# Every feed-forward part opens with a plain pair of gate and up tiles; the ys copy and the next sums go ahead of splits

## Chip, core and metric

The kernel runs on one core of a Trainium2 chip. The metric is the time of one launch on the device in microseconds (us). Three timed runs of the kernel before gave 2052.0, 2054.82 and 2058.25 us, median 2054.82 us.

## What is computed

Two layers act on a hidden state of 512 tokens by 1024 channels, f32. In each layer four parts are added to it, and an RMS norm ends the whole:

```python
h += 1/2 * SwiGLU_1(rmsnorm(h))        # feed-forward, 1024 -> 2816 -> 1024
u  = rmsnorm(h) @ w_in                 # mixer: RG-LRU, windowed attention, gated DeltaNet
h += concat(A, B, C) @ w_out
h += 1/2 * SwiGLU_2(rmsnorm(h))        # second feed-forward
h += sigmoid(rmsnorm(h) @ w_ple_gate) * (p[l] @ w_ple_proj)

def rms_norm(x, g):
    y = x * rsqrt(mean(x * x, axis=-1) + EPS)
    return y * g

def swiglu(x, w_gate, w_up, w_down):
    return (silu(x @ w_gate) * (x @ w_up)) @ w_down
```

There are thus four feed-forward parts: F1 and F2 of layer 0, F1 and F2 of layer 1.

## The kernel before

The hidden state stays in SBUF, transposed, as `hT`: eight tiles of 128 channels by 512 tokens, called d = 0 to 7 here and taken in the order PAIRED = 0, 4, 1, 5, 2, 6, 3, 7. Products are as precise as f32: each operand is split into a high part (rounded to fp32r by ScalarE, ACT) and a low part (the rest, by VectorE, DVE), and each product takes three matmuls: high x high, high x low, low x high. The norm's factor per token is applied after the products; the gain is multiplied in at the split (`gained`, L247).

**A feed-forward part** (`ffn`, L357) makes 22 units: for each of 11 blocks of 256 hidden channels one gate unit (g) and one up unit (u). A unit (`Unit`, L537) is a 2x2 block product by Strassen-Winograd's scheme: seven block products p2, p1, p3, p7, p6, p4, p5 in place of eight, of 4 x 3 = 12 matmuls of 256 columns each, so 84. It needs sums of blocks on both sides. The sums of the weights (s2, s4, and one made by an accumulating DMA from GpSimd's queue into `r`) and their splits, in four groups a, b, c, d, are made by ACT and DVE while the unit before runs. The sums of hT's blocks ("t1", "t2", "T3", "T4", "B22") are made once for each part by `upper` (L272) and `lower` (L285), as hT's tiles get their last value: in the mixer for F2 and in `ple` for F1 of layer 1. So the tail of the stage before makes all operands, and the first pair (`first_pair`, L630) is a Strassen pair whose first products need the last tile of hT after 18 matmuls of 256 columns.

F1 of layer 0 opens otherwise, with `plain_pair` (L692): four plain tiles (g0, g1, u0, u1) of 24 matmuls of 512 columns, that need only the splits of hT, into X tiles; the sums, and the squares for the norm, which DVE adds up in `acc` (L308), follow behind.

PSUM tile Y of a unit holds p3 and p7; p4 adds to its half. ACT must have copied Y to `ys` (p37, L556) before p4 starts on TensorE (PE), and `e` (p16, L560) before p5, which runs inside the next unit. Each engine executes its own list in order. Within a part's rounds PE, ACT and DVE have the order in which the code stands (`manual_schedule`), with splits of down weights between them where a scheduler put them. Round 0 covers blocks 0 to 4 and round 1 blocks 5 to 10; after a round come the down products (pd), whose weights are split in `chunk` and `end`. A round's last unit has no unit to prepare; it loads and splits the first two chunks (`made[0]`, `made[1]`).

The gating of a pair (`Gating`, L480) is spread over the next units: scale (DVE), silu (ACT), mult (DVE), hi (ACT), lo (DVE). Weights of the next part are started early by the generator `ahead`: each `next(ahead)` in the mixer (L879) and in `ple` (L1578) runs one piece of the next part's opening. At the very end `out` multiplies by the norm's row, in part on GpSimd (POOL).

Of the kernel before, what the change touches and what calls it, by code (L numbers as in the profile page):

```python
# [9 lines left out]
F32 = mybir.dt.float32  # L10
# [31 lines left out]


AT0 = (-1, 2)
AT1 = (7, 11)
# [17 lines left out]
def trunk(ctx: ExitStack, tc: tile.TileContext, a):  # L63
# [168 lines left out]
    class Norm:  # L232


        def __init__(self, gain, combined):
            self.gain = gain
            self.acc = per.tile([128, S], F32, tag="acc", name="acc")
            self.x = None
            if combined:
                self.x = Combined()  # L240
                self.raw = {}
                self.neg = per.tile([128, KD], F32, tag="neg", name="neg")
                V.tensor_scalar(out=self.neg, in0=gain, scalar1=-1.0, scalar2=None, op0=ALU.mult)
# [10 lines left out]
        def split(self, k, t512, cs=ALL):  # L254
            if not self.x:
                self.gained(k, cs, self.xh[k][:, cs], self.xl[k][:, cs])
            elif k < 4:
                if cs.stop == S:
                    self.plain(k, cs)
                    self.upper(k, t512)  # L260
            else:
                self.plain(k, cs)
                self.lower(k - 4, cs)

        def plain(self, k, cs=ALL):
            x = self.x
            if k < 4 and hasattr(x, "first"):
                for i in range(2):
                    A.activation(out=x(i, "B11", k), in_=x.first[k][:, i, H:S].bitcast(F32), func=AF.Copy)
            elif k < 4:  # L270
                self.gained(k, HALVES[1], x(0, "B11", k), x(1, "B11", k))
            else:  # L272
                self.gained(k, cs, x.both(0, 0, k - 4)[:, cs], x.both(1, 0, k - 4)[:, cs])

        def upper(self, q, t512):
            x, h, gk = self.x, hT[:, q, :], self.gain[:, q:q + 1]
            g, t14, t32 = t512("tg"), t512("t14"), t512("t32")
            self.raw[q] = g, t14, t32
            A.activation(out=g[:, 0:H], in_=h[:, 0:H], func=AF.Copy, scale=gk)
            V.scalar_tensor_tensor(out=t14[:, 0:H], in0=h[:, H:S], scalar=gk, in1=g[:, 0:H],  # L280
                                   op0=ALU.mult, op1=ALU.subtract)
            split(t14[:, 0:H], x(0, "t1", q), x(1, "t1", q))

        def lower(self, q, cs=ALL):
            x, h = self.x, hT[:, q + 4, :]  # L285
            gk, nk = self.gain[:, q + 4:q + 5], self.neg[:, q + 4:q + 5]
            g, t14, t32 = self.raw[q]
            if cs.start == 0:

                V.scalar_tensor_tensor(out=t32[:, 0:H], in0=h[:, 0:H], scalar=gk, in1=g[:, 0:H],  # L290
                                       op0=ALU.mult, op1=ALU.subtract)
                V.scalar_tensor_tensor(out=t32[:, H:S], in0=h[:, 0:H], scalar=nk, in1=t14[:, 0:H],
                                       op0=ALU.mult, op1=ALU.subtract)
                split(t32, x.both(0, 1, q), x.both(1, 1, q))
            if cs.stop == S:

                V.scalar_tensor_tensor(out=t14[:, H:S], in0=h[:, H:S], scalar=nk, in1=t32[:, H:S],
                                       op0=ALU.mult, op1=ALU.subtract)
                split(t14[:, H:S], x(0, "T4", q), x(1, "T4", q))

        def square(self, k, t512, cs=ALL):
            h, acc = hT[:, k, cs], self.acc[:, cs]
            if k == 0:
# [6 lines left out]
        def add(self, k, t512):  # L310
            if k == 0:
                self.take_operand()
            self.split(k, t512)
            self.square(k, t512)

        def sums(self, t512, cs=ALL):
            n = (cs.stop - cs.start) // 128
            ps = bank([128, NT, 2], "ssc")
            for t in range(n):
# [9 lines left out]
            for x in (rh, rl):  # L329
# [4 lines left out]
                dg = t512("sq", F32R)[:, cs]  # L334
# [22 lines left out]
    def ffn(l, which, at=AT1):  # L357
        with ExitStack() as es:
# [37 lines left out]
            def load(u):  # L396
                j, m = units[u]
                src = a[f"{m}{which}"][l, j]
                if u not in raw1:
                    raw1[u] = loaded(src[:, 0:8], 8)  # L400
                    if u:
                        raw3[u] = wrp.tile([128, 8, 128], F32, tag="wr", name="wr")
                    else:

# [1414 lines left out]
```

## Time and profile before

| | |
|---|---|
| profiled execution, whole | 2052.92 us |
| its span, first to last instruction | 2051.1 us |
| timed runs, median of 3 | 2054.82 us |
| PE busy | 1967.7 us, 96% |
| DVE busy | 1509.4 us, 74% |
| ACT busy | 1002.0 us, 49% |

PE is the bound nearly everywhere. To read on: where PE has idle time, what it waits for, and what in ACT's or DVE's list stands ahead of that. Records of PE overlap: a matmul's record is longer than the step from its start to the next start, so steps are taken from starts.

### The profile page before, as it was taken

Reading aid. Unit: us, or ns where it says so; the run is one execution under the profiler, and the core shown is the slowest. Engines: PE = TensorE matmul, PEld = TensorE weight load, DVE = VectorE, ACT = ScalarE, POOL = GpSimd, SP = SyncE. Lnnn points to the kernel's source line nnn. Section 1 sums busy time; section 2 is a strip of 40 time slices with the busy share of each in tenths; the row PEclk is TensorE's granted clock in tenths of the full one; section 3 lists DMA queues with packets and bytes.
Section 4 is the critical chain, followed back from the end, with each engine's and each line's share of the span. In section 5 each row is a group of like instructions: output and inputs, shape, how many; then the busy total and the mean of one; then the engine's idle time right before and its main releaser. Section 6 shows DMA issues by size and latency. Waiting matters only on the chain.

```text
span 2051.1 us, 32033 instructions
## 1 busy us (share of the span) xinstructions
PE 1967.7 (96%) x12625; PEld 1752.2 (85%) x12625; DVE 1509.4 (74%) x2620; ACT 1002.0 (49%) x1651; POOL 181.2 (9%) x197
## 2 busy tenths in 40 slices
PE   7999999999999999999989999999899999999996
PEld 5988998887778989997879899988677899899885
DVE  7875883879878856865888568647897887488466
ACT  5642652454745534643556336434366565156343
POOL 0100000042201000000000000000421000000001
PEclk8999999999999999999999999999999999999998
DMA  6763743221046745643457357322111377275411
GB/s 193 194 172 95 188 129 113 78 73 47 17 124 171 188 120 147 174 126 103 124 136 189 114 148 186 124 83 96 53 42 44 117 201 192 76 188 139 136 62 62
DMA packets 85415, 254.51 MB, mean 124 GB/s; under 512 B 9616, under 2 KB 17040, under 8 KB 85008
## 3 DMA queue, kind: packets, MB, share of 16 engines
q1 hardware_dynamic: 72880, 207.36, 31.8%
q0 software_dynamic: 12384, 45.09, 12.5%
q8 instruction: 99, 1.62, 0.3%
q14 instruction: 52, 0.43, 0.1%
HBM read 250.32 MB, written 2.10 MB: 123 GB/s over the span
## 4 chain that ended last, share of the span: by engine, by line
PE 75%; DVE 16%; ACT 4%; issue 3%; DMA 1%; SPq 0%; DVEq 0%; ACTq 0%
PE pu L475 10%; PE pg L475 10%; PE pd L147 8%; PE pd L149 8%; PE qu L475 8%; PE pd L148 8%; PE qg L475 7%; PE pp L147 2%; PE pp L148 1%; PE pp L149 1%; PE ppg L149 1%; PE ppg L148 1%; PE ppg L147 1%; DVE wl L124 1%; DVE gl L443 1%
## 5 line engine op out<-in xcount | busy, mean ns | idle before, releaser
L475 PE MATMUL pu<-T,gh 128*128 128x256 f32 x880 | 159.5, 280 | 0.0
L475 PE MATMUL pg<-T,gh 128*128 128x256 f32 x784 | 144.4, 282 | 9.5 <-ACT T L251 7.5
L443 DVE TENSOR_TENSOR gl<-wr,gh 128x1024 fp32r<-128x1024 f32 x102 | 124.6, 1221 | 26.6 <-ACT gh L438 26.6
L123 ACT ACTIVATE wh<-wr 128x1024 fp32r<-128x1024 f32 (+2 forms) x76 | 77.2, 1015 | 135.1 <-PE pp L148 50.5
L475 PEld LDWEIGHTS pu<-T,gh 128*128 128x128 f32 x880 | 134.7, 188 | 0.0
L129 DVE TENSOR_TENSOR gl<-wr,gh 128x1024 fp32r<-128x1024 f32 x53 | 64.5, 1223 | 93.6 <-ACT gh L128 93.4
L475 PEld LDWEIGHTS pg<-T,gh 128*128 128x128 f32 x784 | 121.2, 189 | 11.1 <-ACT T L251 8.1
L147 PE MATMUL pd<-X,gh 128*128 128x512 f32 x328 | 128.8, 393 | 0.0
L149 PE MATMUL pd<-X,gl 128*128 128x512 f32 x328 | 128.7, 392 | 0.0
L148 PE MATMUL pd<-X,gh 128*128 128x512 f32 x328 | 127.8, 390 | 0.0
L475 PE MATMUL pu<-T,gl 128*128 128x256 f32 x440 | 123.0, 279 | 0.0
L438 ACT ACTIVATE gh<-wr 128x1024 fp32r<-128x1024 f32 x102 | 105.2, 1046 | 19.9 <-PE pd L148 14.0
L128 ACT ACTIVATE gh<-wr 128x1024 fp32r<-128x1024 f32 x53 | 55.8, 1059 | 120.7 <-PE pd L148 95.2
L475 PE MATMUL pg<-T,gl 128*128 128x256 f32 x392 | 110.1, 281 | 0.0
L475 PE MATMUL pg<-T,wh 128*128 128x256 f32 x592 | 107.3, 280 | 2.3 <-DVE cg L554 2.3
L124 DVE TENSOR_TENSOR wl<-wr,wh 128x1024 fp32r<-128x1024 f32 (+2 forms) x64 | 74.1, 1157 | 40.9 <-ACT wh L123 40.2
L147 PE MATMUL pp<-X,wh 128*128 128x512 f32 x240 | 102.1, 425 | 0.0
L438 ACT ACTIVATE sh<-r 128x512 fp32r<-128x512 f32 x80 | 50.6, 632 | 103.6 <-DVE r L455 103.6
L149 PE MATMUL pp<-X,wl 128*128 128x512 f32 x240 | 98.2, 409 | 2.0 <-DVE wl L124 2.0
L443 DVE TENSOR_TENSOR wl<-wr,wh 128x1024 fp32r<-128x1024 f32 x67 | 81.8, 1221 | 23.4 <-ACT wh L438 23.4
L148 PE MATMUL pp<-X,wh 128*128 128x512 f32 x240 | 98.2, 409 | 0.2 <-DVE X L252 0.2
L475 PEld LDWEIGHTS pg<-T,wh 128*128 128x128 f32 x592 | 90.5, 188 | 3.2 <-DVE cg L554 2.9
(477 smaller groups left out, 6048.9 us busy)
## 6 DMA issues: line engine op xcount, KB each, us to landing
wr<-in_d_dram SPq DMA_DIRECT2D x64, 512.0 KB, 3.9
wr<-in_g_dram SPq DMA_DIRECT2D x45, 512.0 KB, 4.3
wr<-in_u_dram SPq DMA_DIRECT2D x45, 512.0 KB, 4.3
r<-in_g_dram SPq DMA_DIRECT2D x43, 512.0 KB, 3.7
r<-in_u_dram SPq DMA_DIRECT2D x43, 512.0 KB, 4.1
r<-in_g_dram POOLq DMA_DIRECT2D x43, 512.0 KB, 7.3
r<-in_u_dram POOLq DMA_DIRECT2D x43, 512.0 KB, 6.9
wr<-in_wi_dram SPq DMA_DIRECT2D x30, 512.0 KB, 3.3
```

The lines of the kernel that those rows point to most:

```text
L123: A.activation(out=hi, in_=raw, func=AF.Copy)
L124: (via or V).tensor_tensor(out=lo, in0=raw, in1=hi.bitcast(F32), op=ALU.subtract)
L128: A.activation(out=hi, in_=x, func=AF.Copy)
L129: V.tensor_tensor(out=lo, in0=x, in1=hi.bitcast(F32), op=ALU.subtract)
L147: T.matmul(out=out, lhsT=wh, rhs=xh, start=start, stop=False)
L148: T.matmul(out=out, lhsT=wh, rhs=xl, start=False, stop=False)
L149: T.matmul(out=out, lhsT=wl, rhs=xh, start=False, stop=stop)
L438: A.activation(out=self.g[n][0], in_=self.of(n)[0], func=AF.Copy)
L443: V.tensor_tensor(out=g[1], in0=raw, in1=g[0].bitcast(F32), op=ALU.subtract)
L475: T.matmul(out=ps, lhsT=l_[:, q, :], rhs=r_, start=start and q == 0 and i == 0, stop=stop and q == 3 and i == 2, skip_group_check=more)
```

## The change

1. All four parts open with `plain_pair`. Its operands are the splits of hT in T tiles; the right half of the columns of d = 0 to 3 stands in "B11", the left in "T4", so these blocks take two matmuls of 256 columns in place of one of 512. The tails of the mixer and of `ple` split the plain weights of the next part's first pair (four groups) and hT; the sums of hT's blocks (`sums_of`) are made inside the pair by DVE and ACT, and the last sum, which takes T4's place, behind its last tile. `first_pair` is gone.
2. In F1 of layer 0 the squares are no longer added by DVE: `summed` adds them on PE, 4 matmuls of 2 columns for each d. In the other parts DVE still adds them.
3. In each unit `p37`, the copy to `ys`, goes ahead of the split of group c; `lo` of the pair goes behind that of group a. In a round's last unit `made[1]` goes behind `e`, and the first `end` is made there.
4. `out` multiplies by pairs of tiles on DVE alone; POOL no longer takes part. A tile named dg of its own holds the norm's diagonal, in place of one shared with sq.

```diff
-            if not self.x: ...
-            elif k < 4:
-                if cs.stop == S:
-                    self.plain(k, cs)
-                    self.upper(k, t512)
+            elif k < 4:
+                for half, name in zip(HALVES, ("T4", "B11")):
+                    if cs.start <= half.start and half.stop <= cs.stop:
+                        self.gained(k, half, self.x(0, name, k), self.x(1, name, k))
...
+        def sums_of(self, q, t14, t512):
+            h, h4, g = hT[:, q, :], hT[:, q + 4, :], t512("tg", q)
...
+            A.activation(out=g[:, 0:H], in_=h[:, 0:H], func=AF.Copy, scale=gk)
+            for out, a_, k, b in ((t14[:, 0:H], h[:, H:S], gk, g[:, 0:H]), (t32[:, 0:H], h4[:, 0:H], g4, g[:, 0:H]),
+                                  (t32[:, H:S], h4[:, 0:H], n4, t14[:, 0:H]), (t14[:, H:S], h4[:, H:S], n4, t32[:, H:S])):
+                V.scalar_tensor_tensor(out=out, in0=a_, scalar=k, in1=b, op0=ALU.mult, op1=ALU.subtract)
+            parts = (t14[:, 0:H], [self.x(i, "t1", q) for i in range(2)]), (t32, [self.x.both(i, 1, q) for i in range(2)])
+            for t, (hi, lo) in parts:
+                A.activation(out=hi, in_=t, func=AF.Copy)
...
+            def last():
+                split(t14[:, H:S], self.x(0, "T4", q), self.x(1, "T4", q))
...
+        def summed(self, k, sq):
+            for t in range(NT):
+                T.matmul(out=self.ps[:, t, :], lhsT=sq[:, 128 * t:128 * t + 128], rhs=ones[:, 0:2],
+                         start=k == PAIRED[0] and t == 0, stop=k == PAIRED[-1], skip_group_check=True)
...
+                tile("g", 0)
+                combine(0)
+                combine(1)
+                more[0][0]()
+                squares(PAIRED[0:2])
+                combine(2)
+                more[1][0]()
+                squares(PAIRED[2:4])
                 w.part("a")
+                tile("g", 1)
+                summed(PAIRED[0:4])
+                combine(3)
+                more[2][0]()
+                squares(PAIRED[4:6])
                 w.s2()
+                more[3][0]()
+                squares(PAIRED[6:8])
                 w.part("b")
+                tile("u", 0)
+                summed(PAIRED[4:8])
                 norm.sums(t512)
                 w.s4()
                 w.part("d")
                 w.part("c")
+                tile("u", 1)
+                for _, last in more:
+                    last()
                 return None, None, PlainGating(ps, into(0, 0))
...
                         unit.p(7)
+                        unit.p37()
                         if w:
                             w.room("c")
                             w.hi("c")
-                        unit.p37()
...
                         unit.p16()
+                        if not w:
+                            made[1] = grouped(raws[1], 8)
...
                         unit.c21()
+                        if not w and r == 0:
+                            make_end(0)
...
-                    for i in range(2):
-                        if k + i < n:
-                            V.tensor_tensor(out=o[:, i, :], in0=hT[:, k + i, cs], in1=pr, op=ALU.mult)
-                        else:
-                            G.tensor_tensor(out=o[:, i, :], in0=hT[:, k + i, cs], in1=rb, op=ALU.mult)
+                    V.tensor_tensor(out=o, in0=hT[:, k:k + 2, cs], in1=pr.unsqueeze(1).to_broadcast([128, 2, S // 2]),
+                                    op=ALU.mult)
```

DVE's list at the seam from the mixer of layer 0 to F2, before, from the last tile of hT (L1571) on. `t_` are sums, `T_` their splits, `acc` the squares.

```order
L1571 TENSOR_TENSOR hT<-hT,pwo 128x512
L129 TENSOR_TENSOR T_6035<-t_6030,T_6034 128x256
L290 SCALAR_TENSOR_TENSOR t_6031<-hT,par,tg 128x256
L292 SCALAR_TENSOR_TENSOR t_6031<-hT,neg,t_6030 128x256
L252 SCALAR_TENSOR_TENSOR T_6072<-hT,par,T_6071 128x512
L297 SCALAR_TENSOR_TENSOR t_6030<-hT,neg,t_6031 128x256
L308 TENSOR_TENSOR acc<-acc,sq 128x512
L129 TENSOR_TENSOR T_6078<-t_6031,T_6077 128x512
L243 TENSOR_SCALAR neg<-par 128x8
L129 TENSOR_TENSOR T_6035<-t_6030,T_6034 128x256
L554 TENSOR_TENSOR cg<-cg,pg 128x256
```

The same place after (the tile's last value is made in L1517; `X_6096` to `X_6099` hold sums, `wl` is a split of the plain pair's weights).

```order
L1517 TENSOR_TENSOR hT<-hT,pwo 128x512
L272 SCALAR_TENSOR_TENSOR X_6099<-hT,par,X_6098 128x256
L272 SCALAR_TENSOR_TENSOR X_6099<-hT,neg,X_6096 128x256
L247 SCALAR_TENSOR_TENSOR T_6076<-hT,par,T_6075 128x512
L272 SCALAR_TENSOR_TENSOR X_6096<-hT,neg,X_6099 128x256
L298 TENSOR_TENSOR acc<-acc,sq 128x512
L272 SCALAR_TENSOR_TENSOR X_6096<-hT,par,X_6098 128x256
L272 SCALAR_TENSOR_TENSOR X_6099<-hT,par,X_6098 128x256
L272 SCALAR_TENSOR_TENSOR X_6099<-hT,neg,X_6096 128x256
L272 SCALAR_TENSOR_TENSOR X_6096<-hT,neg,X_6099 128x256
L279 TENSOR_TENSOR T_5844<-X_6096,T_5843 128x256
L279 TENSOR_TENSOR T_6143<-X_6099,T_6142 128x512
```

Before, the sums that need the last tile (L290, L292, L297) stand around its own split (L252), and the splits of these sums (L129) follow at once. After, its split (L247) comes third, the sums (L272) follow it as part of a longer list, pair of tiles by pair, and the splits of T4 (L129) are not among the rows.

ACT's list in the gate unit of the second pair of F2, layer 0, before: splits (L438), the copy to ys (L558), and silu (L500) of the pair before.

```order
L438 ACTIVATE gh<-r_6365 128x1024
L500 ACT_TABLE_LOAD
L500 ACTIVATE th<-cg 128x512 x2
L553 ACTIVATE cg<-pg 128x256
L438 ACTIVATE sh<-r_6365 128x512
L438 ACTIVATE wh<-wr 128x1024
L438 ACTIVATE gh<-wr 128x1024
L558 ACTIVATE ys<-qg 128x512
L562 ACTIVATE e<-pg 128x256
```

The same after: the copy is L539, splits are L429, silu is L509.

```order
L429 ACTIVATE wh<-r_6344 128x1024
L534 ACTIVATE cg<-pg 128x256
L429 ACTIVATE sh<-r_6344 128x512
L429 ACTIVATE gh<-wr 128x1024
L341 ACTIVATE rb<-prow 128x512
L539 ACTIVATE ys<-qg 128x512
L429 ACTIVATE wh<-wr 128x1024
L509 ACT_TABLE_LOAD
L509 ACTIVATE th<-gs 128x512 x2
L543 ACTIVATE e<-pg 128x256
```

Here the silus and their table load stand behind ys, and one split in place of two stands between sh and ys, with the copy of the norm's row (`rb`).

ACT's list in the last unit of round 0 in F1 of layer 0, before: L128 splits down weights.

```order
L553 ACTIVATE cu<-pu 128x256
L128 ACTIVATE gh<-wr 128x1024
L128 ACTIVATE wh<-wr 128x1024
L128 ACTIVATE sh<-wr 128x512
L558 ACTIVATE ys<-qu 128x512
L562 ACTIVATE e<-pu 128x256
L128 ACTIVATE gh<-wr 128x1024
L128 ACTIVATE sh<-wr 128x512
L128 ACTIVATE gh<-wr 128x1024
```

The same after (L124 splits down weights, L539 copies to ys).

```order
L534 ACTIVATE cu<-pu 128x256
L124 ACTIVATE gh<-wr 128x1024
L539 ACTIVATE ys<-qu 128x512
L543 ACTIVATE e<-pu 128x256
L124 ACTIVATE wh<-wr 128x1024
L124 ACTIVATE sh<-wr 128x512
```

One split of down weights is left between cu and ys; the two that followed it now come behind e.

## Rows read from the trace of the kernel before

**Rows 1.** The page, part 1: engine, busy us (share of the span) x instructions.

```profile
PE 1967.7 (96%) x12625; PEld 1752.2 (85%) x12625; DVE 1509.4 (74%) x2620; ACT 1002.0 (49%) x1651; POOL 181.2 (9%) x197
```

**Rows 2.** Waits of PE: engine line <- releaser: us in total, times, longest us.

```profile
PE qg L475 <- ACT ys L558: 9.3, 8, 2.0
PE qg L475 <- ACT sh L438: 8.6, 1, 8.6
...
PE pg L475 <- ACT T L251: 7.5, 3, 6.3
...
PE qu L475 <- ACT ys L558: 6.6, 5, 1.6
```

**Rows 3.** Timeline, PE, F1 of layer 0: start, us, what [idle before <-releaser].

```profile
9.02 0.80 PE L147 MATMUL pg<-X,gh 128*128 128x512 f32 x1 [3.33 <-ACT gh L128]
...
23.65 0.39 PE L147 MATMUL pu<-X,gh 128*128 128x512 f32 x1
...
34.41 0.40 PE L149 MATMUL pu<-T,wl 128*128 128x512 f32 x1
...
70.18 0.40 PE L475 MATMUL pg<-T,gh 128*128 128x256 f32 x2
```

**Rows 4.** The chain that ended last, two units: start us, us, what.

```profile
70.34 2.83 PE pg L475 x24
...
80.23 2.83 PE pu L475 x24
```

**Rows 5.** Timeline, PE, F2 of layer 0.

```profile
620.04 0.39 PE L475 MATMUL pg<-T,gh 128*128 128x256 f32 x2
...
622.87 0.38 PE L475 MATMUL pg<-T,gh 128*128 128x256 f32 x1 [0.64 <-ACT T L251]
...
653.17 0.39 PE L475 MATMUL qg<-T,wh 128*128 128x256 f32 x1 [2.01 <-ACT ys L558]
...
664.59 0.28 PE L475 MATMUL pg<-T,gh 128*128 128x256 f32 x1
```

**Rows 6.** Timeline, PE, F2 of layer 0: the sums of squares, four matmuls.

```profile
633.08 0.95 PE L321 MATMUL ssc<-cst,acc 128*128 128x2 f32 x8
```

**Rows 7.** Timeline, PE, F1 of layer 1.

```profile
1024.96 0.28 PE L475 MATMUL pg<-T,gh 128*128 128x256 f32 x1
...
1033.44 0.58 PE L475 MATMUL pg<-T,gh 128*128 128x256 f32 x1 [6.28 <-ACT T L251]
...
1078.67 0.28 PE L475 MATMUL pg<-T,gh 128*128 128x256 f32 x1
```

**Rows 8.** Timeline, PE, F1 of layer 0: last unit of round 0, first unit of round 1.

```profile
129.60 0.39 PE L475 MATMUL qu<-T,gh 128*128 128x256 f32 x1 [1.32 <-ACT ys L558]
...
195.24 0.39 PE L475 MATMUL qg<-T,wh 128*128 128x256 f32 x1 [0.39 <-ACT ys L558]
```

**Rows 9.** Timeline, ACT, the same last unit of round 0.

```profile
126.01 1.06 ACT L128 ACTIVATE gh<-wr 128x1024 fp32r<-128x1024 f32 x1 [2.95 <-DMA wr<-in_d_dram]
```

**Rows 10.** Timeline, DVE, F2 of layer 0.

```profile
622.31 0.48 DVE L290 SCALAR_TENSOR_TENSOR t<-hT,par,tg 128x256 f32<-128x256 f32 x1
...
634.62 0.15 DVE L323 TENSOR_SCALAR nv<-ssc 128x4 f32<-128x4 f32 x1
...
638.21 0.41 DVE L565 TENSOR_TENSOR cg<-e,qg 128x256 f32<-128x256 f32 x1
```

**Rows 11.** Groups by line and shape, DVE: xcount | busy us, mean ns | idle before.

```profile
L443 DVE TENSOR_TENSOR gl<-wr,gh 128x1024 fp32r<-128x1024 f32 x102 | 124.6, 1221 | 26.6 <-ACT gh L438 26.6
```

**Rows 12.** Windows: stretch, its us, busy of PE, PEld, DVE, ACT, POOL, PEclk, DMA share, GB/s.

```profile
9.00:15.00 6.00, 5.53 (x12) 3.48 (x13) 6.00 (x10) 5.70 (x9) 0.00 (x0) 0.52 1.02 381
49.00:57.00 8.00, 6.43 (x38) 5.86 (x37) 6.79 (x10) 5.25 (x8) 0.86 (x1) 0.79 0.76 198
185.00:310.00 125.00, 124.61 (x1034) 123.38 (x1033) 100.34 (x129) 70.16 (x100) 6.92 (x8) 1.00 0.58 153
```

**Rows 13.** Timeline, POOL, the end.

```profile
2036.79 4.82 POOL L1646 TENSOR_TENSOR o<-hT,rb 128x256 f32<-128x256 f32 x7 [167.71 <-ACT rb L346]
```

More of the change, by code (lines that the diff above doesn't have):

```diff
@@ L284, in lower @@
[L284 to L299, printed above, removed]
+                for half, name in zip(HALVES, ("T4", "B11")):
+                    if cs.start <= half.start and half.stop <= cs.stop:
+                        self.gained(k, half, self.x(0, name, k), self.x(1, name, k))
+            else:
+                self.gained(k, cs, self.x.both(0, 0, k - 4)[:, cs], self.x.both(1, 0, k - 4)[:, cs])
@@ L476, in product @@
                                  stop=stop and q == 3 and i == 2, skip_group_check=more)
-            count = iter(range(1 << 20))
-            def taken():
-                n = next(count)
-                if n == at[0]:
-                    norm.sums(t512)
-                if n == at[1]:
-                    norm.rows()
             class Gating:
@@ new lines, in plain_pair, with temp, combine, tile @@
+                if first:
+                    load2(2)
+                w = pipe[2] = Weights(2)
+                stock = [t[:, i, :].bitcast(F32) for t in [wide(n) for n in range(4, 8)] for i in range(2)]
+                ps, more, sq = {}, [], {}
+                def temp(name, q):
+                    return stock[{"tg": 4, "t32": 6}[name] + q % 2]
+                def combine(q):
+                    more.append(norm.sums_of(q, stock[q], temp))
+                def tile(m, i):
+                    o = ps[m, i] = bank([128, S], "p" + m)
+                    wh, wl = firsts[m, 8 * i]
+                    for q in range(4):
+                        for j in range(2):
+                            b = 4 * (j if i else 1 - j) + q
+                            xs = [(ALL, x.both(0, 0, q), x.both(1, 0, q))] if j else norm.plain(q)
+                            for cs, xh, xl in xs:
+                                for n, (w_, x_) in enumerate(((wh, xh), (wh, xl), (wl, xh))):
+                                    T.matmul(out=o[:, cs], lhsT=w_[:, b, :], rhs=x_, start=q + j + n + cs.start == 0,
+                                             stop=q == 3 and j == 1 and n == 2, skip_group_check=True)
@@ L729, in chunk, with make_end @@
                     return made[d]
-                made = {}
+                def make_end(e):
+                    raw = wrp.tile([128, 4, 128], F32, tag="wr", name="wr")
+                    for i in range(2):
+                        nc.sync.dma_start(out=raw[:, 2 * i:2 * i + 2, :], in_=src[l, 2 * e + i][:, 8:10, :])
+                    ends[e] = halfgroup()
+                    split(raw, *ends[e])
+                made, ends = {}, {}
                 with tc.manual_schedule(engines=inner):
@@ L803, in ffn @@
                             w.lo("c")
+                        if pair and not last:
+                            pair.mult()
                         unit.p(6)
```

240 lines of the change are left out of this document (67 added, 173 removed).

## The prediction

> **What bounds the kernel now.** I read first the page's totals: TensorE (PE) is busy 1967.7 of the span's 2051.1 us [rows 1], so only its idle time and its own work can move the end. Second, the list of what PE waits for [rows 2]: thirteen waits for the copy to ys, 15.9 us (9.3 + 6.6); one of 8.6 for a split sh; three for a T of the last hT tile, 7.5, of which one is 6.3. Third, the chain that ended last: in the middle of a part it is PE alone, unit after unit, 9.89 us each (from 70.34 to 80.23) [rows 4]. Fourth, PE's timeline around the first pairs, where nearly all of these waits lie [rows 3, 5, 7], and at a round's end [rows 8]; then the lists of ACT and DVE there [rows 9, 10].
>
> I measure each part's opening by one stretch: from the first matmul of its first pair to the first matmul of the third pair. It is 61.2 us in F1 of layer 0 (9.02 to 70.18) [rows 3], 44.6 in F2 of layer 0 (620.04 to 664.59) [rows 5], 53.7 in F1 of layer 1 (1024.96 to 1078.67) [rows 7]. F2 of layer 1 repeats F2 of layer 0 to 0.1 us, and I count it as the same.
>
> Steps of PE at the full clock: 47 steps of 512 columns from 23.65 to 34.41 are 0.229 us each [rows 3]; a unit's 84 steps of 256 columns are 9.89 us, so 0.118 each [rows 4]. A plain pair of 96 matmuls is then 22.0 us, a Strassen pair 19.8.
>
> **Work on PE.** The new plain pair takes two matmuls of 256 columns for each of 512 where the operand is one of d = 0 to 3: half of a tile's 24. The pair is 4 x (12 x 0.229 + 24 x 0.118) = 22.3 us. A stretch after holds 22.3, the second pair's two units 19.8 without their last product (12 x 0.118 = 1.4), two 512-column matmuls for the norm's row, 0.46, and the squares' sums, 8 records that hold PE 0.8 us from 633.08 [rows 6]: 41.9 us. In a part that opened with a Strassen pair the work was 2.5 us less, 39.4. So in three parts the change costs 2.5 us of PE each before any wait is counted.
>
> In F1 of layer 0 the squares are added on PE by 32 f32 matmuls of 2 columns in place of 4. Eight records for four matmuls took 0.8 us [rows 6], so 64 records take about 6.5: work there is 41.9 - 0.8 + 6.5 = 47.6, against 41.7 before. This is a cost on the path, and I give nothing back for the DVE instructions that it saves, as they are in the waits below.
>
> **F1 of layer 0, 61.2 us before.** It held 19.5 us of waits and low clock: 8.64 for sh [rows 2], two waits for ys (1.65 and 1.41, inside the 15.9), a clock of 0.79 in the stretch behind the 8.64 [rows 12], and a start at clock 0.52 [rows 12], with 3.7 us beyond the steps at full clock. The wait for sh came because DVE had the sums for three tile pairs, eight squares and their adds in its list ahead of s2. Those adds are gone from DVE, the sums are spread over four tiles, and s2 comes in the second tile. What is left by replaying both lists with the durations of the rows: the start, 3.7; 1.2 in the first tile, as DVE still makes each low part just ahead of its use; 0.9 for the first ys. So 47.6 + 5.8 = 53.4: -7.8 us. Bounds: with nothing but the start left, 51.3, -9.9; with half of the wait for sh left, 58.2, -3.0.
>
> **F2 of both layers, 44.6 us each.** Before, 5.2 us were waits and the slower steps behind them: 0.64 and 0.65 for the last tile's split, 0.79 later, and 2.01 for ys [rows 5]. In a plain pair the first use of the last tile's split comes after 21 of 24 blocks, 4.9 us behind the pair's start, against 2.1: both waits of 0.6 end. But DVE then gets all sums at once behind the last tile: 29 instructions at 0.48 us [rows 10], 13.9 us, so from about 622 to 636 on the trace's clock of before; then the chain from the squares' sums to nb, 3.6 us (634.62 to 638.21) [rows 10], then s4, two low parts, gl, and T4's four splits: about 646, while PE starts the second pair at 620 + 22.3 + 0.8 = 643.2. The second pair's first unit therefore runs close behind DVE: ys ready at 651.5 where PE wants it at 650.7. I take 0.8 for that and 0.5 for the same in the next unit: 41.9 + 1.3 = 43.2, -1.4 each, -2.8 for two. Bounds for each: all waits gone, -2.7; both ys waits as long as the one of before, 41.9 + 2 x 2.1 = 46.1, +1.5.
>
> **F1 of layer 1, 53.7 us.** Before, 6.28 us for the last T, 0.6 behind it, a low clock after it, and ys again [rows 7]. There `ple` makes the last tile of hT in halves, and its T reaches PE 8.5 us behind the pair's start (1033.44). With the plain pair, 2.8 us later in need, and the splits of the last tile not queued behind sums of the other tiles, I expect the low part at 1031.9 against a need at 1030.1: 1.9 left. With F2's 1.3 behind it: 45.1, -8.6. Bounds: no wait left, 41.9, -11.8; half of the 6.28 and the low clock left, 48.7, -5.0.
>
> **The ys copy in steady units and at a round's end.** Of the thirteen waits for ys, five lie in the stretches above (1.65, 1.41 and three of 2.01: 9.1 us). The eight others, 15.9 - 9.1 = 6.8 us, are four at the end of round 0 and 1 (the first 1.32) and four at the start of round 1 (0.39 each) [rows 8]. At the end of a round ACT has three splits of down weights between cu and ys, of which the first begins at 126.01 after 2.95 us of waiting for its DMA [rows 9], and each takes about 1.06. With one split ahead of ys in place of three, ys comes two splits (2.1 us) earlier: the 1.32 goes. With ys ahead of the split of group c the 0.39 goes. So -6.8; bounds -8 (the slower first steps behind a wait go too) and -3.
>
> Those moves put other work later: hi of group c, made[1], lo of the pair. In a steady stretch of 125 us DVE is busy 100.3 and ACT 70.2 [rows 12], so a unit of 9.89 leaves DVE 1.95 us and ACT 4.3 free, and the biggest piece that moves, gl of 1.22 [rows 11], fits in. I cost that at nothing; what it costs without that cover is the third rival.
>
> **The end.** POOL's seven multiplies took 4.82 us from 2036.79 [rows 13]. After, eight DVE instructions of 512 columns do all 16; a 256-column DVE instruction is 0.41 [rows 10], so of 512 columns some 0.65, and behind the last row four of them, 2.6 us, in place of six of 256, 2.5. I take 0; bounds -1.2 (the diagonal no longer waits for a square's buffer) and +1.3 (four that wait for one another's DMA).
>
> **Sum.** -7.8 - 2.8 - 8.6 - 6.8 + 0 = -26.0. The profiled execution took 2052.92, 1.9 below the median of the runs, 2054.82. So 2026.9 by the profile, 2028.8 as a median of runs. All lower ends: -9.9 - 5.4 - 11.8 - 8 - 1.2 = -36.3, 2018.5. All upper ends: -3 + 3 - 5 - 3 + 1.3 = -6.7, 2048.1.
>
> **Rivals.** First, DVE is later than I replay. The 29 instructions are sums of 256 columns and low parts of 512; at 0.6 us each, half of the 1.22 that 1024 columns take [rows 11], they end 3.5 us later, and the second pair waits that long in each part: 4 x 3.5 = +14, 2042.8. For it: DVE's list is the tightest in my replay. Against it: row by row the sums are 0.48.
>
> Second, the clock. Behind the 8.64 us wait the granted clock was 0.79 for 8 us, and at the kernel's start 0.52 for 6 us [rows 12], the lower of the two levels, 1.2 GHz. If the short stops in the openings keep it there, one tile of 24 matmuls costs 24 x (0.44 - 0.229) = 5.1 us more (0.44 is 0.229 / 0.52), and I give this to one of the tiles: 2033.9. Against it: in F2 the pair follows the out product, in which PE never stops, and of the 0.6 us stops none lowered a step [rows 5]. The Trainium skill, "TensorE: Matmul & The Clock Gate", section "HAM oscillation — how this bites in real kernels", says that bursts of matmuls parted by waits put PE back to the lower level again and again; by it this rival would hold in each opening that still stops, while the rows show it only behind long stops.
>
> Third, the other side: the steady units. In each of 72 units (88 less 8 in first pairs and 8 at a round's end) ACT now makes ys ahead of hi of group c, silu and all behind it. ys waits for p7, so what stood ahead of it and was done early is done after p7. If that makes PE wait 0.44 us for the last group in each unit, as the start of round 1 shows for a copy that comes late (0.39) [rows 8], it is 72 x 0.44 = +32: 2060.6. It decides from 26 / 72 = 0.36 us a unit. For it: DVE is busy 80% there [rows 12]. Against it: group c is needed by p4, 24 matmuls or 2.8 us after p7, and gl takes 1.22.
>
> Fourth, the change doesn't do what it says at the round ends: ys still stands behind a split that waits for a DMA [rows 9], so the waits stay: +6.8, 2035.6.
>
> **How the numbers follow.** Forecast 57%, first rival 14%, second 8%, third 8%, fourth 10%; 3% for a stretch that comes out at its upper ends. A change within 0.3%, some 6 us, can't be told from none. The forecast, the second and the fourth are faster, 75%; of the first 11 of 14 are (its 12 us less than before are beyond 6), the rest counts as the same with the 3%; the third is slower. So 0.86 faster, 0.06 same, 0.08 slower. The range takes the lower ends, and above the first rival and most of the upper ends: 2018 to 2046.
>
> **What would show it.** In the profile after: the four stretches at 53.4, 43.2, 45.1 and 43.2; no wait for sh over 2 us; of the eight small ys waits none over 0.3; a stop near ys in each second pair of under 1 us; pieces of 9.89 us in the middle of a part as now. I am wrong if units between grow (third rival), if PE waits over 2 us for a T or sl in the second pair (first), or if the 64 short records of the squares take other than some 6 us.

## The result, and the profile after

The changed kernel takes 2034.26 us (median of four runs, 2031.3 to 2037.97), the one before 2053.57 in the same comparison: a ratio of 0.9903, 95% interval 0.9876 to 0.9931. That is 19.3 us faster where 26.0 were forecast, and inside the range of 2018 to 2046. The profiled execution took 2031.3 (span 2029.4), 21.6 less than that of before, and the account below is of these two. The page's first part, to be read beside [rows 1]:

```profile
PE 1978.0 (97%) x12657; PEld 1760.0 (87%) x12657; DVE 1492.6 (74%) x2591; ACT 980.8 (48%) x1629; POOL 169.5 (8%) x182
```

The list of what PE waits for (us in total, times, longest us), beside [rows 2]:

```profile
PE qu L466 <- ACT ys L539: 5.5, 6, 1.3
...
PE qg L466 <- ACT ys L539: 2.0, 3, 0.9
PE pg L617 <- DVE T L247: 2.0, 2, 1.1
...
PE pg L617 <- ACT T L246: 0.7, 1, 0.7
```

The list of before has one more line for the splits of the last hT tile:

```profile
PE pg L475 <- DVE T L252: 2.0, 3, 0.7
```

PE is busy 10 us longer and yet ends earlier: the wait of 8.6 for sh is gone, the waits for T fell from 7.5 + 2.0 to 2.7, and those for ys from 15.9 to 7.5. The openings, first matmul of the first pair to that of the third, in PE's timeline (start us, us, what):

```profile
9.12 0.51 PE L617 MATMUL pg<-T,gh 128*128 128x256 f32 x2 [2.41 <-ACT gh L124]
...
25.27 4.83 PE L308 MATMUL ssc<-cst,X 128*128 128x2 f32 x32
29.96 0.77 PE L617 MATMUL pu<-T,gh 128*128 128x256 f32 x2
...
37.60 3.63 PE L308 MATMUL ssc<-cst,X 128*128 128x2 f32 x32
41.09 0.77 PE L617 MATMUL pu<-T,wh 128*128 128x256 f32 x2
...
67.36 0.40 PE L466 MATMUL pg<-T,gh 128*128 128x256 f32 x2
...
612.40 0.40 PE L617 MATMUL pg<-T,gh 128*128 128x256 f32 x2
...
644.06 0.51 PE L466 MATMUL qg<-T,gh 128*128 128x256 f32 x2 [0.57 <-ACT ys L539]
...
654.59 0.50 PE L466 MATMUL qu<-T,wh 128*128 128x256 f32 x2 [0.37 <-ACT ys L539]
...
656.11 0.40 PE L466 MATMUL pg<-T,gh 128*128 128x256 f32 x2
...
1015.20 0.40 PE L617 MATMUL pg<-T,gh 128*128 128x256 f32 x2
...
1020.90 0.49 PE L617 MATMUL pg<-T,gh 128*128 128x512 f32 x1 [0.71 <-ACT T L246]
...
1022.24 0.50 PE L617 MATMUL pg<-T,gh 128*128 128x512 f32 x1 [0.84 <-DVE T L247]
...
1048.56 0.50 PE L466 MATMUL qg<-T,gh 128*128 128x256 f32 x2 [0.85 <-ACT ys L539]
...
1060.18 0.39 PE L466 MATMUL pg<-T,gh 128*128 128x256 f32 x2
```

| | before | forecast | after |
|---|---|---|---|
| F1 of layer 0 | 61.2 | 53.4 | 58.2 |
| F2 (layer 0; layer 1 the same) | 44.6 | 43.2 | 43.7 |
| F1 of layer 1 | 53.7 | 45.1 | 45.0 |
| four round ends, sum of steps at the ys wait | 6.3 | 0.5 | 5.8 |
| four starts of round 1, the same | 2.7 | 0.5 | 0.5 |

Beside these, the products behind each F2 gain 1.05 us in layer 0 (from PE's first of them to F1 of layer 1) and 0.87 in layer 1 (to the end's first sums of squares). PE waited there for acc and does not now:

```profile
974.10 0.27 PE L321 MATMUL ssc<-cst,acc 128*128 128x2 f32 x1 [1.20 <-DVE acc L308]
```

Of two weight splits that stood among the squares in DVE's list there, one now stands behind them; that this took the wait away is read from the lists and not tested. The two mixers are 4.4 us shorter and 1.0 longer. The end, from its first sums of squares (2030.42 before, 2010.59 after) to the last instruction, is 18.8 us in place of 20.6 (18.8 to 19.4 over the runs below that have the new end). The down products lose some 0.2 us eight times. F1 of layer 0 shows where its gain went (columns as in [rows 12]):

```profile
25.27:29.96 4.69, 4.69 (x33) 4.69 (x32) 3.73 (x10) 2.72 (x5) 0.53 (x1) 0.73 0.98 224
29.96:34.34 4.38, 4.38 (x18) 4.03 (x18) 1.93 (x4) 1.58 (x2) 0.00 (x0) 0.51 0.93 189
34.34:37.60 3.26, 3.26 (x22) 2.92 (x21) 0.00 (x0) 0.00 (x0) 0.00 (x0) 1.00 0.03 5
41.09:48.30 7.21, 7.21 (x39) 6.53 (x39) 5.67 (x17) 2.72 (x7) 0.00 (x0) 0.76 0.17 52
```

PE is busy all the time, but while it does the 32 short records the clock falls, and the tile behind starts at 0.51, the 1.2 GHz level. Tiles u0 and u1 take 7.6 and 7.2 us in place of 5.6. The loss differs from profile to profile. In four runs below that leave this opening as it is, it takes 58.5 us (`again`), 56.4 (`ends`), 56.8 (`rep8`) and 56.4 (`tail_old`); over these and the one above, the 64 short records take 7.0 to 8.2 us and the two tiles 2.6 to 4.0 us more than their 11.2. At a round's end ACT's list reads (start us, us, what, idle before):

```profile
119.85 0.38 ACT L534 ACTIVATE cu<-pu 128x256 f32<-128x256 f32 x1 [1.89 <-PE pu L466]
124.98 1.06 ACT L124 ACTIVATE gh<-wr 128x1024 fp32r<-128x1024 f32 x1 [4.75 <-DMA wr<-in_d_dram]
125.94 0.58 ACT L539 ACTIVATE ys<-qu 128x512 f32<-128x512 f32 x1
```

The one split that was left between cu and ys waits 4.75 us for its DMA, and ys behind it. It is that of the third chunk. Before, the row of [rows 9] stood between these:

```profile
122.67 0.38 ACT L553 ACTIVATE cu<-pu 128x256 f32<-128x256 f32 x1 [1.88 <-PE pu L475]
...
128.44 0.63 ACT L128 ACTIVATE sh<-wr 128x512 fp32r<-128x512 f32 x1 [0.42 <-DMA wr<-in_d_dram]
128.97 0.58 ACT L558 ACTIVATE ys<-qu 128x512 f32<-128x512 f32 x1
```

So ys begins 6.1 us behind cu after (125.94 - 119.85) and 6.3 before. The first split behind cu begins 5.1 us behind it after (124.98) and 3.3 before (126.01), because part 3 moved a load too. SyncE (SP) issues these loads, here the one for that split before, and then, after, the two for the early `end` and the one for the third chunk:

```profile
119.52 0.33 SPq L387 DMA_DIRECT2D wr<-in_d_dram  x1
```

```profile
117.03 0.80 SPq L675 DMA_DIRECT2D wr<-in_d_dram  x2
...
119.25 0.33 SPq L382 DMA_DIRECT2D wr<-in_d_dram  x1
```

Before, the load went out 3.2 us ahead of cu; after, it goes out behind the two of the `end`, 0.6 us ahead of cu.

### The profile page after: what moved, and what is told of

It reads as the page before. It is cut to its first block, busy times and chain, and to the rows that moved or that the text cites. A ratio compares the mean times of both kernels' runs of the same rounds, so it can differ in the third digit from the quotient of the medians.

```text
span 2029.4 us, 32039 instructions
## 1 busy us (share of the span) xinstructions
PE 1978.0 (97%) x12657; PEld 1760.0 (87%) x12657; DVE 1492.6 (74%) x2591; ACT 980.8 (48%) x1629; POOL 169.5 (8%) x182
## 4 chain that ended last, share of the span: by engine, by line
PE 87%; DVE 7%; ACT 3%; DMA 2%; issue 1%; SPq 0%; POOL 0%; DVEq 0%; ACTq 0%
PE pu L466 10%; PE pg L466 10%; PE pd L143 8%; PE pd L145 8%; PE pd L144 8%; PE qg L466 8%; PE qu L466 7%; PE pp L143 2%; PE pp L144 2%; PE pp L145 2%; PE pg L617 2%; PE pu L617 2%; PE ppg L143 1%; PE ppg L145 1%; PE pwo L145 1%; PE ppg L144 1%
## 5 line engine op out<-in xcount | busy, mean ns | idle before, releaser
L466 PE MATMUL pu<-T,gh 128*128 128x256 f32 x736 | 133.2, 280 | 0.0
L124 ACT ACTIVATE gh<-wr 128x1024 fp32r<-128x1024 f32 x56 | 59.3, 1059 | 137.6 <-PE pd L144 63.9
L429 ACT ACTIVATE sh<-r 128x512 fp32r<-128x512 f32 x80 | 50.6, 632 | 140.2 <-DVE r L446 140.2
L466 PEld LDWEIGHTS pu<-T,gh 128*128 128x128 f32 x736 | 112.3, 188 | 0.0
L429 ACT ACTIVATE gh<-wr 128x1024 fp32r<-128x1024 f32 x96 | 100.6, 1048 | 23.6 <-PE pd L144 23.6
L466 PE MATMUL pu<-T,gl 128*128 128x256 f32 x368 | 102.9, 280 | 0.0
L143 PE MATMUL pp<-X,wh 128*128 128x512 f32 x240 | 101.6, 423 | 0.0
L143 PE MATMUL pd<-X,gh 128*128 128x512 f32 x256 | 101.2, 395 | 0.0
L143 PE MATMUL pd<-X,wh 128*128 128x512 f32 x256 | 101.2, 395 | 0.0
L145 PE MATMUL pd<-X,gl 128*128 128x512 f32 x256 | 100.6, 393 | 0.0
L145 PE MATMUL pd<-X,wl 128*128 128x512 f32 x256 | 100.6, 393 | 0.0
L434 DVE TENSOR_TENSOR gl<-r,gh 128x1024 fp32r<-128x1024 f32 x52 | 63.7, 1224 | 50.0 <-ACT gh L429 50.0
L144 PE MATMUL pd<-X,gh 128*128 128x512 f32 x256 | 100.0, 391 | 0.0
L144 PE MATMUL pd<-X,wh 128*128 128x512 f32 x256 | 100.0, 390 | 0.0
L466 PE MATMUL pu<-T,wh 128*128 128x256 f32 x544 | 98.2, 280 | 0.0
```

Source lines behind the costliest of these rows:

```text
L124: A.activation(out=hi, in_=x, func=AF.Copy)
L143: T.matmul(out=out, lhsT=wh, rhs=xh, start=start, stop=False)
L144: T.matmul(out=out, lhsT=wh, rhs=xl, start=False, stop=False)
L145: T.matmul(out=out, lhsT=wl, rhs=xh, start=False, stop=stop)
L429: A.activation(out=self.g[n][0], in_=self.of(n)[0], func=AF.Copy)
L434: V.tensor_tensor(out=g[1], in0=raw, in1=g[0].bitcast(F32), op=ALU.subtract)
```

## The experiments

The ratios are against the kernel before, run beside each.

**The changed kernel again** (`again`, no edit).

> The changed kernel once more, unaltered. Its four runs so far lie at 2031.3 (twice) and at 2037.2 and 2038.0. Theory: some 4 us of the mixer's time in layer 0 turn on where the clock happens to be low there, so a second profile shows the feed-forward openings within 0.3 us of the first (58.2, 43.7, 45.0, 43.7) and the mixer of layer 0 different by some us. Rival: all of the 4.4 us that the mixer of layer 0 gained over the kernel before come from the change; then the mixer (369.5 to 565.1) is 195.6 us again. Median expected 2031 to 2038.

Measured 2036.1 us (2029.15 to 2037.88), 0.9901 (0.9880 to 0.9923); profiled 2035.64. The opening of F1 of layer 0 is 0.3 us longer, the other three are the same to 0.1 us. From the first product of the mixer of layer 0 to its out products it took 195.6 us, as in the first profile (195.7; before 200.1), but in layer 1 196.0 against 199.6: over all kernels here, whose mixers are the same, the two read 195.6 to 200.1 with no order. So the 4.4 us can't be credited to the change, and neither the theory nor its rival is shown for layer 0 alone. The second profile is 4.3 us longer all the same, since round 0 of F2 of layer 0 and of F1 of layer 1 take 2.7 and 4.1 us more, for the wait at their ends:

```profile
717.52 0.80 PE L466 MATMUL qu<-T,gh 128*128 128x256 f32 x2 [2.42 <-ACT ys L539]
...
1124.57 0.80 PE L466 MATMUL qu<-T,gh 128*128 128x256 f32 x2 [2.85 <-ACT ys L539]
```

They were 1.26 and 1.20 us in the first profile. Behind the longer ones the first two matmuls take 0.80 us together in place of 0.50: the clock has fallen too (0.52 from 717.5 to 721.0, where the first profile has 1.00 behind its wait).

**The split behind e.** (`ends`)

```diff
                             made[1] = grouped(raws[1], 8)
+                            chunk(2)
```

> In a round's last unit the split of the third chunk of down weights, which stood ahead of the copy to ys and waited for its DMA, is written behind e. Theory: the four waits for ys at the end of round 0 (steps of 1.39, 1.53, 1.47, 1.44 us in place of 0.12) go, 5.3 us in all. Rival: the down products then wait for the same weights, and the first matmuls of pd come no earlier: within 1 us of the changed kernel.

Measured 2026.7 us (2023.53 to 2028.31), 0.9863 (0.9843 to 0.9883): 9.4 us under the changed kernel beside it, and the runs lie closer together. At a round's end PE no longer waits for ys. ACT's row of ys now, which waits for PE alone:

```profile
122.23 0.60 ACT L539 ACTIVATE ys<-qu 128x512 f32<-128x512 f32 x1 [3.86 <-PE qu L466]
```

The theory holds in its cause. Its 5.3 us was too small, as it came from a profile with short waits. From the third pair to the first down product, round 0 takes 60.77 us in all four parts here, and in the three kernels below that have this edit too. In the six profiles with the round ends of the changed kernel it takes 61.6 to 66.2 us, and its four stretches together 5.0 to 13.4 us more than here. That fits a gain of 9.4, and this range of 8.4 us is about as wide as the scatter of the changed kernel's runs here, 8.7 us. The rival fails: the down products took one step of 0.68 us, once.

**Squares on DVE.** (`sq_dve`). `norm.ps` stays empty, so `square` adds into acc, and four matmuls sum acc.

```diff
-                    if first:
+                    if norm.ps:
...
-    norm.ps = bank([128, NT, 2], "ssc")
```

> Part 2 of the change undone alone: in F1 of layer 0 DVE adds the squares into acc, as in the other parts, and PE has 4 matmuls of 2 columns in place of 32. Theory (the 64 short records cost their own time, 8.2 us against 0.8, and they take the clock to half in the tiles behind them, 3.8 us): opening 58.2 - 7.4 - 3.8 = 47 us, if DVE's seven adds of 0.6 us fit in its idle 8.2 us; with some of them late 47 to 50. So 8 to 11 us faster than the changed kernel. Rival (DVE was the bound, which is why the sums went to PE): the wait for sh returns, at 4 us or more, and the gain is below 5 us.

Measured 2035.21 us, 0.9903 (0.9882 to 0.9924), no different from the changed kernel as a whole. Its profile has 9.3 us of ys waits at the round ends, where the first profile of the changed kernel has 4.7; in that profile this takes back what the opening gains. The opening is 10.00 to 63.81, 53.8 us, so 4.4 less than 58.2 and 2.5 to 4.7 less over the profiles with the short matmuls, and not 11. The reason is in PE's timeline:

```profile
35.29 1.86 PE L316 MATMUL ssc<-cst,acc 128*128 128x2 f32 x8 [3.67 <-DVE acc L298]
```

The rival is the better account: DVE is late with the adds, PE stops 3.67 us, and u1 behind the stop runs at a clock of 0.69 in the mean (37.0 to 44.7) and takes 7.7 us. It is a wait for acc, though, not for sh.

**Short matmuls spread.** (`spread`). In tile u0, four short ones behind each block, in place of two runs of 16. In this kernel the squares of the last four d are added twice and those of the first four not at all; the number of matmuls is the same.

```diff
+                            if between:
+                                between([PAIRED[2 * q + j]])
...
-                tile("u", 0)
-                summed(PAIRED[4:8])
+                tile("u", 0, summed)
```

> The same 32 short matmuls, but 4 of them behind each of the 8 blocks of tile u0 in place of two runs of 16. Theory (a run of short matmuls in one piece lowers the clock): the clock stays at 1.0, and the opening is 4 to 5 us shorter, 53 to 54. Rival (the clock falls by the share of short matmuls, wherever they stand, or for another reason such as the start): opening 57 to 61, clock still near 0.5 in part of u0 or u1.

Measured 2042.99 us, 0.9946 (0.9927 to 0.9965): 7 us slower than the changed kernel beside it. Opening 67.9 us, 9.6 more than in the first profile (1.7 of it a wait for the squares ahead of the first short matmuls). That wait, and windows over most of u0 (in two) and over u1:

```profile
27.17 1.18 PE L308 MATMUL ssc<-cst,X 128*128 128x2 f32 x8 [1.69 <-ACT X L291]
```

```profile
28.50:40.00 11.50, 11.50 (x50) 10.92 (x49) 1.73 (x2) 1.13 (x2) 0.00 (x0) 0.50 0.40 81
40.00:49.00 9.00, 9.00 (x38) 8.42 (x37) 0.00 (x0) 0.00 (x0) 0.00 (x0) 0.50 0.00 0
49.00:57.40 8.40, 8.40 (x38) 7.59 (x38) 6.74 (x21) 2.92 (x6) 0.00 (x0) 0.63 0.28 90
```

The theory is refuted: with the short matmuls mixed in, the clock is at the lower level (0.50) from 28.5 to 49.0 us, with PE busy throughout. The rival's low clock is there, over a longer stretch than it said (opening 67.9, not 57 to 61). As a stop of 1.7 us stands ahead of the fall, this run does not tell what took the clock down; the next one does.

**Eight times the sums** (`rep8`) in the three other openings.

```diff
-            for t in range(0 if self.ps else n):
+            for t in range(0 if self.ps else n) if not self.x else [t for _ in range(8) for t in range(0 if self.ps else n)]:
```

> The three openings that add squares on DVE make their four sums of 2 columns eight times over (64 short records in place of 8; the result is the same). At full clock this is 56 x 0.11 = 6.1 us for each opening. Theory (a stretch of short matmuls takes the clock down): tile u1 behind them takes 1.5 to 2.5 us more than its 5.5 us, the short ones themselves over 7 us, clock near 0.5 to 0.8 there; openings of F2 51 to 53 us against 43.7. Rival (what lowered the clock in F1 of layer 0 was the kernel's start, or the stops before it): clock stays 1.0, openings 49.8.

One run: 2064.85 us. The openings of F2 take 52.0 and 51.8 us, as the theory says (the rival said 49.8), that of F1 of layer 1 55.1. F2 of layer 0, windows over u0, the short records (in two) and u1:

```profile
627.00:632.40 5.40, 5.40 (x37) 4.90 (x36) 4.49 (x9) 1.58 (x2) 0.00 (x0) 1.00 0.00 0
632.60:637.00 4.40, 4.40 (x42) 4.39 (x40) 0.00 (x0) 0.00 (x0) 0.00 (x0) 1.00 0.00 0
637.00:641.20 4.20, 4.20 (x26) 4.20 (x25) 0.00 (x0) 0.00 (x0) 0.00 (x0) 0.60 0.00 0
641.30:648.40 7.10, 7.10 (x37) 6.45 (x38) 5.53 (x17) 2.58 (x6) 0.00 (x0) 0.76 0.14 46
```

PE has no stop from the start of this opening (615.73) to the end of the short records. The clock falls while PE is busy with nothing but short matmuls: 1.00 from 632.6 to 637.0, and 0.60 from 637.0 to 641.2. Behind them u1 takes 7.2 us (641.33 to 648.55), as in F1 of layer 0. The theory is shown.

**Part 3 undone** (`order_old`): p37 behind hi of c, mult and lo in their old places, made[1] ahead of p3, and no early first `end`.

```diff
+                        if not w:
+                            made[1] = grouped(raws[1], 8)
                         unit.p(3)
...
-                        unit.p37()
                         if w:
                             w.room("c")
                             w.hi("c")
+                        unit.p37()
...
-                        if not w and r == 0:
-                            make_end(0)
```

> Part 3 of the change undone alone: hi of group c ahead of ys again, mult and lo of the pair in their old places, made[1] ahead of p3 and no early first end. Theory (part 3 is worth the four waits at the start of round 1, some 0.55 us each, and part of the ys waits in the second pairs; at round ends it brought nothing): steps of 0.67 us at each start of round 1 again, ys steps in the second pairs 0.5 to 1.5 us longer than 0.85 and 0.65, in all 4 to 9 us slower than the changed kernel, 2038 to 2045. Rival (part 3 costs as much in steady units as it gives): within 2 us of the changed kernel.

Measured 2045.72 us, 0.9946 (0.9931 to 0.9961): 9 us slower than the changed kernel by the ratios. The steps of 0.67 are back at the four starts of round 1 (2.2 us), and each F2 stops longer for ys:

```profile
649.10 0.51 PE L466 MATMUL qg<-T,gh 128*128 128x256 f32 x2 [1.51 <-ACT ys L539]
...
660.68 0.51 PE L466 MATMUL qu<-T,wh 128*128 128x256 f32 x2 [1.41 <-ACT ys L539]
...
724.03 0.80 PE L466 MATMUL qu<-T,gh 128*128 128x256 f32 x2 [3.72 <-ACT ys L539]
```

Against 0.57 and 0.37 above, that is 2 us for each F2. The last row is a round's end, 3.72 here; the three others wait 1.2 to 1.8 us. The four stretches of round 0 together take 10.6 us more than in `ends`, inside the range of 5.0 to 13.4, so at the round ends part 3 shows no gain. In F1 of layer 0 the load for the split behind cu goes out at 117.45, 3.2 us ahead of cu (120.60) again, so it was part 3 that moved it. So part 3 is worth what the theory says, at its upper end, and costs nothing in steady units.

The opening of F2 of layer 0 is 45.7 us here (616.49 to 662.21), over the 44.6 of the kernel before, and that of F1 of layer 1 46.1. In F2 the plain pair without part 3 is thus a loss of 1.2 us (45.72 against 44.55), and part 3 makes it a gain; in F1 of layer 1 the plain pair without part 3 brings 7.6 of the 8.7 us.

**The old end** (`tail_old`; part 4 undone, the diagonal's own tile kept).

```diff
-                    V.tensor_tensor(out=o, in0=hT[:, k:k + 2, cs], in1=pr.unsqueeze(1).to_broadcast([128, 2, S // 2]),
-                                    op=ALU.mult)
+                    for i in range(2):
+                        if k + i < n:
+                            V.tensor_tensor(out=o[:, i, :], in0=hT[:, k + i, cs], in1=pr, op=ALU.mult)
+                        else:
+                            G.tensor_tensor(out=o[:, i, :], in0=hT[:, k + i, cs], in1=rb, op=ALU.mult)
```

> The end's multiplies undone alone: POOL takes seven tiles of the first half and two of the second, as before; the diagonal keeps its own tile. Theory (the changed end gains 1 us over the one before, from the diagonal's own tile, as ACT's square no longer waits for it): the end is then the same within 0.5 us as in the changed kernel. Rival (POOL's multiplies slow DVE's short instructions in the last chain): the last chain to the norm's row is 0.5 to 2 us longer, and the whole by as much.

Measured 2035.55 us, 0.9909 (0.9896 to 0.9922); the whole does not tell it from the changed kernel. The last wait for the norm's row does: 6.11 us here, 4.83 in the changed kernel (5.51 before). From its first sums of squares (2012.22) the end takes 20.6 us, as before the change. DVE's chain beside POOL's multiplies:

```profile
2018.77 0.47 DVE L152 TENSOR_SCALAR ni<-nv 128x2 int32<-128x2 int32 x1
2019.27 0.65 DVE L154 TENSOR_SCALAR ny<-ni 128x2 int32<-128x2 int32 x1
...
2023.35 0.16 DVE L163 TENSOR_TENSOR nb<-nb,nv 128x2 f32<-128x2 f32 x1
```

Instructions of 0.16 us take 0.65 until POOL is done. The rival is shown: the gain at the end, 1.8 us in the first profile and 1.2 at the least, came from POOL's silence. The diagonal's own tile, which this kernel keeps, does not shorten the end.

**Three edits together** (`best`): the split behind e, squares on DVE, and in F1 of layer 0 the sums behind u1. The code of the third:

```diff
-                norm.sums(t512)
+                if not first:
+                    norm.sums(t512)
                 w.s4()
...
                 tile("u", 1)
+                if first:
+                    norm.sums(t512)
```

> Three edits on the changed kernel: the split of the third chunk behind e at a round's end (as in ends), the squares of F1 of layer 0 added on DVE (as in sq_dve), and there the norm's sums behind tile u1 in place of ahead of it, so that PE does u1 while DVE ends its adds. Theory (in sq_dve PE stopped 3.67 us for acc and ran at half clock for part of u1 behind that stop; both go): opening of F1 of layer 0 46.5 to 49 us, against 58.2 in the changed kernel and 53.8 in sq_dve; whole kernel 5 to 10 us under ends, 2017 to 2022. Rival (the chain from the sums to the norm's row, 3.6 us, and T4's splits behind it are then late for the second pair): a new stop at prow or in the second pair of 2 us or more, opening 50 to 52.

Measured 2019.81 us (2018.5 to 2022.95), 0.9831 (0.9819 to 0.9844): the fastest here, 34.9 us under before. That is inside the theory's range for the whole. The opening is 10.29 to 62.56, 52.3 us, where the theory said 46.5 to 49 and the rival 50 to 52. So the rival is the better account of it, though no stop reaches its 2 us: u0 and u1 run at clock 1.00, but the chain to the norm's row stands ahead of the next pair's work in DVE's list:

```profile
43.20 0.47 PE L339 MATMUL prow<-dg,ones_r 128*128 128x512 f32 x1 [0.54 <-DVE rl L328]
...
47.32 0.50 PE L466 MATMUL pg<-T,gh 128*128 128x256 f32 x2 [1.50 <-DVE cg L535]
50.50 0.51 PE L466 MATMUL qg<-T,gh 128*128 128x256 f32 x2 [1.50 <-ACT ys L539]
```

**The same with the adds on POOL** (`best_pool`), and that with the sums ahead of u1 as in the changed kernel (`pool_early`).

```diff
-                V.tensor_tensor(out=acc, in0=acc, in1=sq, op=ALU.add)
+                (G if self.pool else V).tensor_tensor(out=acc, in0=acc, in1=sq, op=ALU.add)
```

> As best, but the seven adds of squares in F1 of layer 0 are POOL's, which stands idle there, in place of DVE's. Theory (the stops in best's opening, 0.5 at prow and 1.5 us twice in the second pair, come from DVE's list, which is 2 to 3 us late there; seven adds of 0.6 less take 4 us off it): the two stops of 1.5 us fall to under 0.5, opening 48 to 50 in place of 52.3, whole 2 to 4 us under best. Rival (POOL's work slows DVE's beside it, as in the kernel's end, and its adds hold up the accumulating DMAs in its queue, so that r comes late for s2): opening 52 or more.

> As best_pool, but the norm's sums ahead of tile u1, where the changed kernel has them. Theory (POOL needs 7 adds of some 1.4 us, two of 256 columns taking that at the kernel's end, from about 20 on, so acc is there at 31 to 34): PE stops 0 to 2.5 us ahead of u1; if it does not stop, the chain is early and the opening is 47 to 49; if it stops, 50 to 53, since the clock falls too. Rival as in best_pool.

Measured 2024.22 us, 0.9851 (0.9837 to 0.9865), and 2026.18 us, 0.9861 (0.9846 to 0.9876). By the medians they are 4.4 and 6.4 us slower than the three edits; the first one's interval still overlaps with theirs. Openings 55.2 and 56.7 us, where the theories said 48 to 50 and at most 53. An add takes POOL 1.7 to 2.3 us, and some of DVE's work beside it takes twice as long or more. The first of the two kernels, POOL and then DVE:

```profile
30.96 7.34 POOL L299 TENSOR_TENSOR acc<-acc,X 128x512 f32<-128x512 f32 x4 [1.61 <-ACT X L298]
```

```profile
33.04 1.27 DVE L239 TENSOR_SCALAR neg<-par 128x8 f32<-128x8 f32 x1
...
34.82 2.33 DVE L435 TENSOR_TENSOR gl<-r,gh 128x1024 fp32r<-128x1024 f32 x1
```

The split gl is 1.22 us alone [rows 11], and the row of neg takes 0.17 in `best`. In the second kernel PE stops 6.22 us for POOL's acc. So the rival holds in its first half, POOL's work slowing DVE's. Its second half, that r comes late for s2, does not show: the sum that needs r starts 22.1 us behind the opening's start here (30.99) and 22.2 in `best`. The Trainium skill, "SBUF — State Buffer", section "SBUF: two separate sides", says that GpSimd and VectorE share a port pair as an exclusive lock, which blocks the loser for the whole of the other's instruction. The old end agrees: DVE takes one step each 0.68 us there, and POOL's seven multiplies 0.69 each (4.82 in all, as in [rows 13]). The rows of this kernel are in keeping with it, but do not show one instruction waiting for one.

## Why the prediction was right or wrong

The terms of the sum gave 16 of the 26.0 us that it forecast: F1 of layer 0 3.0, F1 of layer 1 8.7, the two F2 1.8, the round ends 0.5 and the starts of round 1 2.2. The profiles differ by 21.6 all the same, as places that the sum put at nothing gave some 5.5 more, 3.4 of them scatter in the mixers. That the whole came out so near to the forecast is luck to that extent.

**F1 of layer 1 and F2: right.** 45.0 against 45.1, 43.7 against 43.2. In F1 of layer 1 the wait of 6.28 is gone. The 1.9 that the sum left for the last tile's split is there in two steps of 0.99 and 1.34 us, and of the two stops for ys the first alone. In F2 the plain pair makes PE work 2.5 us more and takes away the waits for the last tile; the two stops for ys stand where the replay of DVE's list put them, with steps of 0.85 and 0.65 us. The sum did not tell the plain pair from part 3 here: by `order_old` the plain pair alone would lose, and the gain is part 3's. No run undoes the plain pair alone; what it is worth in F1 of layer 1 is read from the waits.

**F1 of layer 0: -3.0 in place of -7.8.** The step that failed is "64 records take about 6.5: work there is 41.9 - 0.8 + 6.5". The records took 8.2 (4.69 + 3.49), which the prediction itself had named as a sign of being wrong, and the two tiles behind them 3.6 us more, because the short matmuls lower the clock; `rep8` shows the cause. Over five profiles the records took 7.0 to 8.2, so at the full clock 6.5 was near, and it is the clock that the step lacked. The stop of 0.9 for ys was 0.1 instead. The upper bound of 58.2 is what was measured, but by chance: it stood for half of the wait for sh, which came to nothing, and with that half alone it would be 57.7 (53.4 + 4.3). The second rival had the clock fall, with this part among its places, but behind stops; its price of 5.1 us was near, its cause was not this. Nor would the other choice, DVE, have given 11 us: `sq_dve` gained 4.4.

**Round ends: 0.5 in place of 5.2.** The fourth rival, at 10%, came true: "ys still stands behind a split that waits for a DMA". The step that failed is "With one split ahead of ys in place of three, ys comes two splits (2.1 us) earlier". It counted the splits ahead of ys and held the start of the first where [rows 9] has it, 3.3 us behind cu. But the last of the three splits waited for a load too, and part 3 made the third chunk's load go out behind the two of the `end`, so that the one split that is left starts 5.1 us behind cu, and ys came 0.2 us earlier and not 2.1. Fewer splits are worth nothing while the one that is left arrives last. `ends` shows that the wait goes when this split leaves the place ahead of ys. All four of these waits lie at the end of round 0; the prediction also names round 1, where there is none.

**Starts of round 1: right**, 2.2 us gained. **Steady units: right**, no cost: from the start of round 1 of F1 of layer 0 to its down products it is 118.6 us (184.86 to 303.49), before 119.5 (187.62 to 307.08), and 0.55 of that is the wait at the start. The third rival is refuted. The first rival did not happen.

**The end: -1.8 in place of 0**, by POOL's effect on DVE's chain, which `tail_old` shows. The sum counted the multiplies and not what POOL's do to DVE's instructions beside them; the bound of -1.2 stood for the diagonal's tile.

**Not forecast**: 1.9 us in the products behind the two F2, read from the traces and not tested; some 1.8 us lost in the down products, of which the cause stays open; and 3.4 us net in the mixers, which is scatter.

## What to carry to other kernels

When an edit takes one of several instructions from ahead of a critical copy, look at what each of them waits for: only the last arrival counts. Look also at which loads the edit moves in their queue. Moving sums to TensorE as many matmuls of two columns costs their time and the clock of the tiles behind; count both. An idle GpSimd is not free capacity where VectorE is the engine that runs late.

## What the runs showed of the hardware

While PE did nothing but matmuls of 2 columns, busy without a gap, the granted clock fell to 1.2 GHz (a mean of 0.60 over the last 4.2 us of 64 records, 1.00 over the 4.4 us ahead of these), and with four of them behind each block of a tile it stayed there (0.50 from 28.5 to 49.0 us, PE busy throughout). The Trainium skill, "TensorE: Matmul & The Clock Gate", section "HAM oscillation — how this bites in real kernels", ties the fall to long gaps in PE's work, and not, as the prediction took it, to any stop; here it came without one, so the measurement decides. VectorE's instructions of 0.16 us took 0.65 beside GpSimd's multiplies, and a split of 1.22 us took 2.33.
